# A decoder trunk on one core: another order for the opening of the projection

## The chip, the core and the metric

The kernel runs on one core of a Trainium2 chip. The core has a matrix engine (TensorE, PE in the profile), a vector engine (VectorE, DVE), an activation engine (ScalarE, ACT), GpSimd (POOL), and SyncE (SP), which here only issues DMAs. Each engine takes its own instructions in order and waits on semaphores for the others. Matrix results land in PSUM, of which the kernel uses eight banks of 128 x 512 numbers; all else is in SBUF, 128 partitions wide. The metric is the time of one execution on the device in microseconds (us); less is better.

## What is computed

One layer of a decoder trunk in float32. There are 1024 prompt tokens and 32 sample tokens (8 sequences of 4), 1056 in all, with 1024 features. Shortened from the reference:

```
h = x * rsqrt(mean(x*x) + eps) * norm_g              # RMSNorm, per token
b, c, u, z_a, v, z_b = split(h @ w_in)               # six parts of 512 columns
cu = c * u
y_a = b * conv3(cu) * silu(z_a)                      # short causal convolution, 3 taps
pooled = mean of the last 2/4/8/16 tokens of v - v   # four groups of 128 channels
y_b = (pooled @ pool_w) * pool_scale * silu(z_b)
x = x + concat(y_a, y_b) @ w_out
y = x * rsqrt(mean(x*x) + eps) * final_g
```

The last rows of cu and of v are given back as new states.

## The kernel before

**Layout.** In the projection, channels lie on partitions and the 1056 tokens along the free axis, in three column groups n0, n1, n2 of 352. The input x arrives transposed as raw[0], raw[1], raw[2], one tile for each group, with eight chunks of 128 features. RMSNorm's factor is one number per token, so it is not put on x: the projection takes the raw x, and its result is multiplied by R, a 128 x 1056 tile that holds the factor of each token in every partition (R2 is its square, for the product c * u).

**Three passes.** Every float32 operand is split into a high part (copied by ScalarE, type fp32r) and a low part (source minus high, by VectorE). A product is high x low + low x high + high x high, so a weight chunk takes three matmuls. `split` and `split2` (L153, L154) do this for x and for weights.

**Pairs.** The 24 blocks of 128 output channels are done as twelve pairs. Pair 0 (v and z_b of group 0) goes by plain matmuls, `project_first` (L188), into six banks pm[i, n] while x is still arriving. Each later pair p uses a Strassen-like scheme over n0 and n1 in `strassen`: blocks of twelve matmuls (`block`, L228) with the weight blocks B11, B21, B12, B22 and their combinations T1 to T4, against pieces of x (A11, A12, A22) and sums of them (S1 to S4). n2 is done plainly, into banks l and r. For pair 1 the tiles of the sums must first be made from raw[0] and raw[1] (S1f, S3f, S2f, S4f), and they take the buffers of raw_2 (S1), A21 (S3), raw_1 (S2) and raw_0 (S4). Weights are prepared pair by pair: `load_w` (DMA), `gain_w` (times norm_g, L202), `make_t` (T combinations, L207 to L209), and `make_unit` a (B11, B21), b (B12, B22), c (T1, T3) and d (T2, T4), each a split of 128 x 1024.

**The token factor.** The squared sums ss of the tokens come in two ways. For tokens 0 to 639, x is loaded once more with tokens on partitions (xk, five loads of 128 rows, `square`), and ScalarE squares and sums each row (`square2`, L239). For the other 416 tokens, `squares_head` and `squares_last` square raw[1] and raw[2] and add the chunks up in acc, and `sums_rest` sums over partitions with 128 x 1 matmuls (`rest`, L266), each copied into ss by ScalarE (L267). `rows` makes the inverse root (L274 to L280) and a diagonal tile diag of nine pieces (L285), and `rows_out` spreads it over the partitions with matmuls against ones (pr, L292) and copies it to R (L293) and R2 (L294). The heads of pair 0, in vb and szb, are multiplied by R from their banks (L531, L533).

**Order.** In the opening, a block marked `manual_schedule` fixes the order of PE, ACT, DVE and POOL among its own instructions, as they are written. All later instructions, and SP's queue throughout, are ordered by a planner: it plays the program through with estimated durations and lets each engine take the ready instruction that stands first in the program. Instructions written after the block can be placed between instructions of the block where its next one is not ready. The tile pools give buffers out by name: `tmp` has eight, the PSUM pool eight banks; an instruction that needs a buffer waits until all users of the one before are done.

After the projection the mixed rows go through w_out (L613, L685) and the final norm.

Of the kernel before, what the change touches and what calls it, by code (L numbers as in the profile page):

```python
# [7 lines left out]
F32 = mybir.dt.float32  # L8
# [5 lines left out]
P = 128  # L14
D = 1024
# [47 lines left out]
def trunk(ctx, tc, xt, xres, xct, w_first, w_in, w_out, pool_w, par, fg, sconv, spool,  # L63
# [166 lines left out]
                             skip_group_check=True)  # L230


    def square(t):
        xk = tp.tile([P, D], F32, tag="tmp", name=f"xk_{t}")
        nc.sync.dma_start(xk, xres[t * P:(t + 1) * P])
        return xk

    def square2(t, xk):
        nc.scalar.activation(xk, xk, AF.Square, accum_out=ss[:, t:t + 1])  # L239


# [6 lines left out]
        vt(sh[:, :2], sh[:, :2], sh[:, 2:4], op=ADD)  # L248
        vt(acc[:, :REST], sh[:, 0], sh[:, 1], op=ADD)

    def squares_last(acc):
        for k in range(0, KD, 2):
            sq = tmp(f"sq_{k}")
            nc.scalar.activation(sq[:, :2 * TN].rearrange("p (k c) -> p k c", k=2), raw[2][:, k:k + 2], AF.Square)
            if k == 0:
                vt(acc[:, REST:TC], sq[:, :TN], sq[:, TN:2 * TN], op=ADD)
            else:
                vt(sq[:, :TN], sq[:, :TN], sq[:, TN:2 * TN], op=ADD)
                vt(acc[:, REST:TC], acc[:, REST:TC], sq[:, :TN], op=ADD)

    def sums_rest(acc):
        pt = bank("rest")
# [6 lines left out]
    def rows():  # L269

        ms = sm.tile([P, NTOK], F32, tag="ms", name="ms")
        r = sm.tile([P, NTOK], F32, tag="r0", name="r0")
        u = sm.tile([P, NTOK], F32, tag="u0", name="u0")
        nc.vector.tensor_scalar(ms, ss, 1.0 / D, EPS, op0=ALU.mult, op1=ALU.add)  # L274
        nc.scalar.activation(u, ms, AF.Sqrt)
        nc.vector.reciprocal(r, u)
        nc.vector.tensor_tensor(u, ms, r, op=ALU.mult)
        nc.vector.tensor_tensor(u, u, r, op=ALU.mult)
        nc.vector.tensor_scalar(u, u, -0.5, 1.5, op0=ALU.mult, op1=ALU.add)
        nc.vector.tensor_tensor(r, r, u, op=ALU.mult)  # L280
        diag = tmp("diag")
        nc.vector.memset(diag[:, SEQ:], 0.0)
        for t in range(NTOK):
            m = min(P, TOK - t * P)
            nc.vector.tensor_scalar(diag[:m, t * P:t * P + m], ident[:m, :m],  # L285
                                    r[:m, t:t + 1], None, op0=ALU.mult)
        return diag

# [105 lines left out]

    def strassen(p, S1, S2, S3, S4, hooks):
        (q, j), (_, _) = PAIRS[p]
        if q == "v":
            left = vb[:, PM:]
            right = szb[j] = tmp(f"szb_{j}")
            scale = R  # L400
        elif q == "c":
            left, right = tmp(f"t_{j}"), tmp(f"um_{j}")
            scale = R2
        else:
            left, right = tmp(f"z_{j}"), tmp(f"y_{j}")
            scale = R
        n0, n1, n2 = cols

        def plain(i, name):
            pt = bank(name)[:, :TN]  # L410
            block(pt, p, ("B11", "B12")[i], pl[0], True, False)
            block(pt, p, ("B21", "B22")[i], pl[1], False, True)
            return pt

        a = bank(f"a_{p}")[:, :TN]
        block(a, p, "B11", A11, True, False)
        s1 = snap(f"s1_{p}")
        nc.scalar.copy(s1, a)
        if hooks.get("first"):
            block(a, p, "B21", A12, False, True)  # L420
            vt(left[:, n0], a, scale[:, n0], op=MUL)
            hooks["first"]()
        b = bank(f"b_{p}")[:, :TN]
        block(b, p, "T2", S2, True, False)
        t1 = snap(f"t1_{p}")
        vt(t1, b, s1, op=ADD)  # L426
        c = bank(f"c_{p}")[:, :TN]
        block(c, p, "T1", S1, True, False)
        if "plain" in hooks:
            pL, pR = hooks["plain"]  # L430
        else:
            pL = plain(0, f"l_{p}")
        vt(left[:, n2], pL, scale[:, n2], op=MUL)
        hooks["early"]()
        if not hooks.get("first"):
            block(a, p, "B21", A12, False, True)
            vt(left[:, n0], a, scale[:, n0], op=MUL)
        block(b, p, "T3", S3, False, False)
        t2 = snap(f"t2_{p}")
        vt(t2, b, s1, op=ADD)  # L440
        vt(right[:, n1], c, t2, op=ADD)
        if "plain" not in hooks:
            pR = plain(1, f"r_{p}")
        if q == "v":
            vt(right[:, n2], pR, R[:, n2], op=MUL)
        elif q == "c":
            vt(up[:, 2 + 2 * TN:], pR, left[:, n2], op=MUL)
        else:
            nc.scalar.copy(right[:, n2], pR)
        hooks["middle"]()  # L450
        block(b, p, "T4", A22, False, True)
        vt(left[:, n1], b, s1, op=ADD)
        gt(left[:, n1], left[:, n1], scale[:, n1], op=MUL)
        block(c, p, "B22", S4, False, True)
        vt(right[:, n0], c, t1, op=ADD)
        hooks["late"]()

        if q == "v":
            after_v(j)
            gt(right[:, both], right[:, both], R[:, both], op=MUL)  # L460
            silu(right)
        elif q == "c":
            gt(up[:, 2:2 + 2 * TN], right[:, both], left[:, both], op=MUL)
# [11 lines left out]
    with tc.manual_schedule(engines={ET.PE, ET.Activation, ET.DVE, ET.Pool}):  # L475
        for k in range(KD):
            prep_w0(k)
            split_x(2, k, 1)
            project_first(2, k)
        nc.vector.tensor_copy(gain.rearrange("p (k o) -> p k o", o=1), wfraw[:, :, 2 * P:])  # L480
        load_w(1)
        nc.sync.dma_start(part, par)
        sq = [square(t) for t in range(NTT)]
        for n in (0, 1):
            for k in range(0, KD, 2):
                split_x(n, k, 2)
            for k in range(KD):
                project_first(n, k)
        for i in range(2):
            nc.scalar.copy(heads[i][:, n2], pm[i, 2])  # L490
        acc = tmp("acc")
        squares_head(acc)
        gain_w(1)
        make_unit(1, "a")
        make_unit(1, "b")
        squares_last(acc)
# [3 lines left out]
        vt(S3f, raw[0][:, :KH], raw[1][:, :KH], op=ALU.subtract)  # L500
        S1 = xtile("xa", "S1")
        split(S1, S1f)
        S3 = xtile("xb", "S3")
        split(S3, S3f)
        for t in range(NTT):
            square2(t, sq[t])
        vt(S2f, S1f, raw[0][:, :KH], op=ALU.subtract)
        S4f = [tp.tile([P, 2, TN], F32, tag="tmp", name=f"S4f_{h}") for h in range(2)]
        for h in range(2):
            vt(S4f[h], raw[0][:, KH + 2 * h:KH + 2 * h + 2], S2f[:, 2 * h:2 * h + 2], op=ALU.subtract)  # L510
        S2 = xtile("xc", "S2")
        split(S2, S2f)
        make_t(1)
        make_unit(1, "d")
        pL = bank("l_1")[:, :TN]
        block(pL, 1, "B11", pl[0], True, False)
        block(pL, 1, "B21", pl[1], False, True)
        pR = bank("r_1")[:, :TN]
        block(pR, 1, "B12", pl[0], True, False)
        block(pR, 1, "B22", pl[1], False, True)  # L520
        sums_rest(acc)
        diag = rows()
        rows_out(diag)
# [4 lines left out]
        make_unit(1, "c")  # L528
        for n in (0, 1):
            for i in range(2):  # L530
                vt(heads[i][:, cols[n]], pm[i, n], R[:, cols[n]], op=MUL)  # L531
        for i in range(2):
            gt(heads[i][:, n2], heads[i][:, n2], R[:, n2], op=MUL)  # L533
    nc.sync.dma_start(scb[:, :, 0:2 * NB], sconv)
    nc.sync.dma_start(spb[:, :, 0:15 * NB], spool)
    pwraw = tmp("pwraw")[:, :NG * P].rearrange("p (g c) -> p g c", c=P)
    nc.sync.dma_start(pwraw, pool_w)

    linear = {}
    for p in range(1, NP):  # L540
# [17 lines left out]

        hooks = {"early": early, "middle": middle, "late": late}
        if p == 1:  # L560
            def first():
                split(pws, pwraw)
                after_v(0)
                silu(szb[0])

            hooks["plain"] = (pL, pR)
            hooks["first"] = first
        strassen(p, S1, S2, S3, S4, hooks)
        if PAIRS[p - 1][0][0] == "v":
            pool_linear(PAIRS[p - 1][0][1])  # L570
    nc.sync.dma_start(npool_p, npp)
# [213 lines left out]
```

## Time and profile before

| | |
|---|---|
| median of 3 runs | 401.23 us (399.94 to 402.31) |
| the profiled execution | 399.92 us |
| its span, first to last instruction | 397.9 us |
| mean granted TensorE clock | 0.967 |
| busy: PE, DVE, ACT, POOL | 371.4, 268.7, 174.1, 42.0 us |
| moved by DMA | 41.68 MB |

How to read the rows. A row of the timeline has the start in us, the duration in us, the engine, the line, the operation, the tile written and the tiles read, their sizes, and the count; a bracket gives the idle time of the engine just before and the instruction that ended it. Instructions that follow each other closely are merged in one row with their count. A row of a stretch has its limits, its length, then busy time and count of PE, PEld (weight loads), DVE, ACT and POOL, the granted clock as a part of full speed, the share of the DMA engines, and GB/s. A row of the waits has who waited for whom: us in all, times, the longest. PEclk on the page is the granted clock in tenths, in 40 slices of 9.95 us. The bracketed idle time of an engine matters only where that engine holds up the end.

### The profile page before, as it was taken

The page shows a single profiled execution, that of the slowest core. Times are in us where ns is not written, and L with a number is a line of the kernel's source. Part 1 is how long each engine was busy: PE and PEld are TensorE (multiplying, and loading weights), DVE is VectorE, ACT ScalarE, POOL GpSimd, SP SyncE. Part 2 cuts the span into 40 slices and gives each one's busy share as a digit, 9 for nine tenths or more (in the row PEclk, how much of TensorE's full clock was granted, in tenths as well). Part 3 has the DMA queues.
Part 4 walks back from the last instruction along what each step waited for, and adds up shares of the span by engine and source line. Part 5 has one row for each costly group of instructions (what it writes and reads, how often), then busy time and mean ns, then how long its engine had stood idle before and what let it go on. Part 6 is the DMA issues. An engine that isn't in the chain of part 4 may idle for free.

```text
span 397.9 us, 5295 instructions
## 1 busy us (share of the span) xinstructions
PE 371.4 (93%) x2114; PEld 353.8 (89%) x2114; DVE 268.7 (68%) x404; ACT 174.1 (44%) x297; POOL 42.0 (11%) x31
## 2 busy tenths in 40 slices
PE   9998058899999999999999999999999999999993
PEld 6898038899999999999999999999997889999883
DVE  4858848977587887657887766678339908322593
ACT  5884649425442545453353536163137606111211
POOL 0000001041003032000202200303301000000000
PEclk9999559899999999999999999999999999999999
DMA  7980030040402022040204041030808951400042
GB/s 221 413 308 0 1 133 0 0 161 0 161 0 100 7 77 85 2 160 2 105 2 160 0 152 38 24 136 5 321 6 279 413 225 53 161 0 2 1 171 105
DMA packets 13368, 41.68 MB, mean 105 GB/s; under 512 B 3744, under 2 KB 4896, under 8 KB 11936
## 3 DMA queue, kind: packets, MB, share of 16 engines
q1 hardware_dynamic: 13200, 41.02, 28.2%
q8 instruction: 16, 0.26, 0.3%
q10 hardware_dynamic: 144, 0.33, 0.2%
q14 instruction: 8, 0.07, 0.0%
HBM read 32.92 MB, written 8.42 MB: 104 GB/s over the span
## 4 chain that ended last, share of the span: by engine, by line
PE 74%; DVE 11%; ACT 7%; DMA 4%; issue 2%; SPq 1%; POOL 1%; DVEq 0%; ACTq 0%; POOLq 0%
PE b L228 14%; PE po L613 13%; PE pc L685 9%; PE r L228 9%; PE c L228 9%; PE a L228 9%; PE l L228 9%; DMA raw<-in_xt_dram 4%; PE pp L369 2%; DVE win L347 2%; ACT wraw L202 2%; ACT xk L239 1%; PE pr L292 1%; DVE tw L207 1%; DVE wa L154 1%
## 5 line engine op out<-in xcount | busy, mean ns | idle before, releaser
L613 PE MATMUL po<-wo,mix 128*128 128x512 f32 (+1 forms) x264 | 56.7, 375 | 0.2 <-DVE mix L154 0.2
L613 PEld LDWEIGHTS po<-wo,mix 128*128 128x128 f32 x264 | 46.2, 188 | 10.2 <-DVE mix L154 0.9
L228 PE MATMUL a<-A,wa 128*128 128x352 f32 x264 | 47.5, 329 | 0.0
L228 PEld LDWEIGHTS a<-A,wa 128*128 128x128 f32 x264 | 44.2, 192 | 0.6 <-ACT R L293 0.4
L228 PE MATMUL l<-pl,wa 128*128 128x352 f32 x264 | 44.5, 324 | 0.0
L228 PE MATMUL r<-pl,wb 128*128 128x352 f32 x264 | 44.5, 324 | 0.0
L202 ACT ACTIVATE wraw<-wraw,gain 128x256 f32<-128x256 f32 x88 | 36.7, 497 | 17.4 <-DMA wraw<-in_w_in_dram 16.4
L228 PEld LDWEIGHTS l<-pl,wa 128*128 128x128 f32 x264 | 43.0, 188 | 0.0
L228 PEld LDWEIGHTS r<-pl,wb 128*128 128x128 f32 x264 | 43.0, 188 | 0.0
L685 PE MATMUL pc<-mix,wo 128*128 128x416 f32 x192 | 36.5, 352 | 0.0
L685 PEld LDWEIGHTS pc<-mix,wo 128*128 128x128 f32 x192 | 35.9, 188 | 0.5
L207 DVE TENSOR_TENSOR tw<-wraw 128x1024 f32<-128x1024 f32 x11 | 14.1, 1280 | 20.9 <-ACT wraw L202 20.9
L228 PE MATMUL b<-S,wc 128*128 128x352 f32 x132 | 24.4, 336 | 2.6 <-DVE t L426 2.6
L153 ACT ACTIVATE wd<-tw 128x1024 fp32r<-128x1024 f32 x11 | 11.7, 1060 | 33.1 <-DVE tw L209 33.1
L228 PEld LDWEIGHTS b<-S,wc 128*128 128x128 f32 x132 | 22.6, 196 | 2.8 <-DVE t L426 2.8
L228 PE MATMUL b<-A,wd 128*128 128x352 f32 x132 | 23.2, 325 | 0.1
L228 PE MATMUL c<-S,wc 128*128 128x352 f32 x132 | 23.3, 324 | 0.0
L228 PE MATMUL b<-S,wd 128*128 128x352 f32 x132 | 23.1, 324 | 0.0
L228 PE MATMUL c<-S,wb 128*128 128x352 f32 x132 | 23.1, 324 | 0.0
L228 PEld LDWEIGHTS b<-A,wd 128*128 128x128 f32 x132 | 21.6, 188 | 0.4 <-DVE t L440 0.4
L228 PEld LDWEIGHTS c<-S,wc 128*128 128x128 f32 x132 | 21.7, 188 | 0.0
L228 PEld LDWEIGHTS b<-S,wd 128*128 128x128 f32 x132 | 21.7, 188 | 0.0
(173 smaller groups left out, 549.2 us busy)
## 6 DMA issues: line engine op xcount, KB each, us to landing
wraw<-in_w_in_dram SPq DMA_DIRECT2D x11, 1024.0 KB, 4.7
woraw<-in_w_out_dram SPq DMA_DIRECT2D x8, 512.0 KB, 5.9
raw<-in_xt_dram SPq DMA_DIRECT2D x4, 704.0 KB, 9.2
xk<-in_xres_dram SPq DMA_DIRECT2D x5, 512.0 KB, 10.8
zt<-in_xres_dram SPq DMA_DIRECT2D x5, 512.0 KB, 6.8
spill_b<-yb SPq DMA_DIRECT2D x4, 528.0 KB, 3.7
mixraw<-spill_b SPq DMA_DIRECT2D x4, 528.0 KB, 5.6
out_yt_dram<-zt SPq DMA_DIRECT2D x4, 512.0 KB, 2.8
```

The source lines that it names most:

```text
L153: nc.scalar.activation(hi, src, AF.Copy)
L154: nc.vector.tensor_tensor(lo, src, hi.bitcast(F32), op=ALU.subtract)
L202: nc.scalar.activation(t, t, AF.Copy, scale=gain[:, k:k + 1])
L207: nc.vector.tensor_tensor(t[:, 0:2], w[:, 2:4], w[:, 0::2], op=ALU.subtract)
L228: nc.tensor.matmul(pt, t[:, a, i, k * P:(k + 1) * P], x[:, b, k], start=first and s == 0, stop=last and s == len(seq) - 1, skip_group_chec ...
L239: nc.scalar.activation(xk, xk, AF.Square, accum_out=ss[:, t:t + 1])
L292: nc.tensor.matmul(pt, ones, diag[:, cols[n]], start=True, stop=True)
L347: nc.vector.tensor_tensor(o[:, lo2:PM + SEQ], a[:, lo2:PM + SEQ], a[:, lo2 - s:PM + SEQ - s], op=ALU.add)
L369: nc.tensor.matmul(pt[:, :TN], pws[:, a, g, :], pooled[g][b][:, cols[n]], start=(s == 0), stop=(s == 2))
L613: nc.tensor.matmul(pt, mix[k][:, b, t * P:(t + 1) * P], wo[k][:, a, c], start=(k == 0 and s == 0), stop=(k == KD - 1 and s == 2))
L685: nc.tensor.matmul(pt, wo[k][:, a, d * P:(d + 1) * P], mix[k][:, b, T0:], start=(k == 0 and s == 0), stop=(k == KD - 1 and s == 2))
```

## The change

It concerns the opening and pair 1 alone:

- The sums S1f and S3f come right after the splits of x, and S1, unit c and S3 ahead of S2 and unit d.
- `squares_head` stands ahead of the last x split; `squares_last` squares in three pieces into three buffers, and the additions (`sums_last`) are written after the manual block.
- The row squares are written after the block. Their first three loads go into R, R2 and up, which are not in use yet; the fifth is issued later.
- The banks of pair 0 are copied out unscaled by ScalarE, all six, and GpSimd multiplies the two heads by R in place, 1056 columns each.
- GpSimd makes diag instead of VectorE.
- The first bank of pair 1, a (24 matmuls), joins l and r (48) ahead of the column sums, inside the manual block; c with T1 is written ahead of b with T2.
- `sums_rest`, `rows` and `rows_out` are written after the block, and so are ordered by the planner.
- Splitting pool_w is written ahead of pair 1; `after_v(0)` and silu of szb[0] behind it.

```diff
+    def load_rows(t):
+        xk = {0: R, 1: R2, 2: up[:, 2:]}[t] if t < 3 else tmp(f"xk_{t}")
+        nc.sync.dma_start(xk[:, :D], xres[t * P:(t + 1) * P])
+        return xk[:, :D]
+    def square_rows(t, xk):
         nc.scalar.activation(xk, xk, AF.Square, accum_out=ss[:, t:t + 1])
...
+    def squares_last():
+        sq = []
+        for k in range(0, KD, 3):
+            t = tmp(f"sq_{k}").rearrange("p (k c) -> p k c", c=TN)[:, :min(3, KD - k)]
+            nc.scalar.activation(t, raw[2][:, k:min(k + 3, KD)], AF.Square)
+            sq.append(t)
+        return sq
+    def sums_last(acc, sq):
+        out = acc[:, REST:TC]
+        vt(sq[0], sq[0], sq[1], op=ADD)
+        vt(sq[0][:, :2], sq[0][:, :2], sq[2], op=ADD)
+        vt(out, sq[0][:, 0], sq[0][:, 1], op=ADD)
+        vt(out, out, sq[0][:, 2], op=ADD)
...
-        nc.vector.memset(diag[:, SEQ:], 0.0)
+        nc.gpsimd.memset(diag[:, SEQ:], 0.0)
...
-            nc.vector.tensor_scalar(diag[:m, t * P:t * P + m], ident[:m, :m],
+            nc.gpsimd.tensor_scalar(diag[:m, t * P:t * P + m], ident[:m, :m],
...
+        if p == 1:
+            a, s1, pL, pR = hooks["open"]
...
+        if p == 1:
+            block(c, p, "T1", S1, True, False)
         block(b, p, "T2", S2, True, False)
...
-        sq = [square(t) for t in range(NTT)]
+        xk = [load_rows(t) for t in range(4)]
+        acc = tmp("acc")
         for n in (0, 1):
             for k in range(0, KD, 2):
                 split_x(n, k, 2)
+                if (n, k) == (1, 4):
+                    squares_head(acc)
             for k in range(KD):
                 project_first(n, k)
...
         vt(S1f, raw[1][:, :KH], raw[1][:, KH:], op=ADD)
         vt(S3f, raw[0][:, :KH], raw[1][:, :KH], op=ALU.subtract)
+        gain_w(1)
+        make_unit(1, "a")
+        for i in range(2):
+            nc.scalar.copy(heads[i][:, n2], pm[i, 2])
+        sq = squares_last()
         vt(S2f, S1f, raw[0][:, :KH], op=ALU.subtract)
+        make_unit(1, "b")
         S4f = ...
+        make_t(1)
+        S1 = xtile("xa", "S1")
+        split(S1, S1f)
+        make_unit(1, "c")
+        S3 = xtile("xb", "S3")
+        split(S3, S3f)
+        for n in (0, 1):
+            for i in range(2):
+                nc.scalar.copy(heads[i][:, cols[n]], pm[i, n])
         S2 = xtile("xc", "S2")
         split(S2, S2f)
         make_unit(1, "d")
         S4 = xtile("xd", "S4")
...
+        pL, pR = plain1(0), plain1(1)
+        a1 = bank("a_1")[:, :TN]
+        block(a1, 1, "B11", A11, True, False)
+        s1 = snap("s1_1")
+        nc.scalar.copy(s1, a1)
+        block(a1, 1, "B21", A12, False, True)
+    sums_last(acc, sq)
+    xk.append(load_rows(4))
+    for t in range(NTT):
+        square_rows(t, xk[t])
+    sums_rest(acc)
+    diag = rows()
+    rows_out(diag)
+    for i in range(2):
+        gt(heads[i], heads[i], R, op=MUL)
...
+    split(pws, pwraw)
...
         strassen(p, S1, S2, S3, S4, hooks)
+        if p == 1:
+            after_v(0)
+            silu(szb[0])
```

More of the change, by code (lines that the diff above doesn't have):

```diff
@@ L230, in block @@
                              skip_group_check=True)
[L233 to L238, printed above, removed]
+    def load_rows(t):
[3 more added lines that the diff above has]
+    def square_rows(t, xk):
         nc.scalar.activation(xk, xk, AF.Square, accum_out=ss[:, t:t + 1])
@@ L249, in squares_head @@
         vt(acc[:, :REST], sh[:, 0], sh[:, 1], op=ADD)
[L251 to L259, printed above, removed]
+    def squares_last():
[11 more added lines that the diff above has]
+        vt(out, out, sq[0][:, 2], op=ADD)
     def sums_rest(acc):
@@ L413, in plain @@
             return pt
[L415 to L422, printed above, removed]
+        if p == 1:
+            a, s1, pL, pR = hooks["open"]
+        else:
+            a = bank(f"a_{p}")[:, :TN]
+            s1 = snap(f"s1_{p}")
+            block(a, p, "B11", A11, True, False)
+            nc.scalar.copy(s1, a)
         b = bank(f"b_{p}")[:, :TN]
+        c = bank(f"c_{p}")[:, :TN]
+        if p == 1:
+            block(c, p, "T1", S1, True, False)
         block(b, p, "T2", S2, True, False)
@@ L426, in strassen @@
         vt(t1, b, s1, op=ADD)
[L427 to L431, printed above, removed]
+        if p > 1:
+            block(c, p, "T1", S1, True, False)
+        if p > 1:
             pL = plain(0, f"l_{p}")
@@ L434, in strassen @@
         hooks["early"]()
-        if not hooks.get("first"):
+        if p > 1:
             block(a, p, "B21", A12, False, True)
-            vt(left[:, n0], a, scale[:, n0], op=MUL)
+        vt(left[:, n0], a, scale[:, n0], op=MUL)
         block(b, p, "T3", S3, False, False)
@@ L441, in strassen @@
         vt(right[:, n1], c, t2, op=ADD)
-        if "plain" not in hooks:
+        if p > 1:
             pR = plain(1, f"r_{p}")
@@ L486, in trunk @@
                 split_x(n, k, 2)
+                if (n, k) == (1, 4):
+                    squares_head(acc)
             for k in range(KD):
                 project_first(n, k)
[L489 to L496, printed above, removed]
         S1f, S3f, S2f = raw[1][:, KH:], raw[1][:, :KH], raw[0][:, :KH]
@@ L500, in trunk @@
         vt(S3f, raw[0][:, :KH], raw[1][:, :KH], op=ALU.subtract)
[L501 to L506, printed above, removed]
+        gain_w(1)
[3 more added lines that the diff above has]
+        sq = squares_last()
         vt(S2f, S1f, raw[0][:, :KH], op=ALU.subtract)
+        make_unit(1, "b")
         S4f = [tp.tile([P, 2, TN], F32, tag="tmp", name=f"S4f_{h}") for h in range(2)]
@@ L510, in trunk, with plain1 @@
             vt(S4f[h], raw[0][:, KH + 2 * h:KH + 2 * h + 2], S2f[:, 2 * h:2 * h + 2], op=ALU.subtract)
+        make_t(1)
+        def plain1(i):
+            pt = bank(f"lr{i}_1")[:, :TN]
+            block(pt, 1, ("B11", "B12")[i], pl[0], True, False)
+            block(pt, 1, ("B21", "B22")[i], pl[1], False, True)
+            return pt
+        S1 = xtile("xa", "S1")
[6 more added lines that the diff above has]
+                nc.scalar.copy(heads[i][:, cols[n]], pm[i, n])
         S2 = xtile("xc", "S2")
         split(S2, S2f)
-        make_t(1)
         make_unit(1, "d")
[L515 to L523, printed above, removed]
         S4 = xtile("xd", "S4")
@@ L527, in trunk @@
             split2(S4[:, 0, ks], S4[:, 1, ks], S4f[h])
[L528 to L533, printed above, removed]
+        pL, pR = plain1(0), plain1(1)
[13 more added lines that the diff above has]
+        gt(heads[i], heads[i], R, op=MUL)
     nc.sync.dma_start(scb[:, :, 0:2 * NB], sconv)
@@ L560, in trunk @@
         if p == 1:
[L561 to L567, printed above, removed]
+            hooks["open"] = (a1, s1, pL, pR)
         strassen(p, S1, S2, S3, S4, hooks)
+        if p == 1:
+            after_v(0)
+            silu(szb[0])
         if PAIRS[p - 1][0][0] == "v":
```

## The prediction, made before the changed kernel ran

> **What bounds the kernel now.** I read the page's engine and slice tables first, then busy time by stretch, TensorE's waits, and the timeline of each engine from 14 to 82 us.
>
> ```profile
> span 397.9 us, 5295 instructions
> ...
> PEclk9999559899999999999999999999999999999999
> ```
> ```profile
> 38.60:80.10 41.50, 23.00 (x106) 20.25 (x107) 32.73 (x57) 26.13 (x47) 1.86 (x2) 0.71 0.09 32
> 80.10:330.00 249.90, 249.59 (x1484) 242.78 (x1483) 175.59 (x226) 106.61 (x168) 38.73 (x22) 1.00 0.29 104
> ```
> ```profile
> PE rest L266 <- ACT ss L267: 13.3, 3, 12.8
> PE b L228 <- DVE t L426: 2.6, 1, 2.6
> PE pr L292 <- DVE diag L285: 2.5, 1, 2.5
> ```
> ```profile
> 34.55 4.04 PE L228 MATMUL r<-pl,wb 128*128 128x352 f32 x24
> 55.94 3.89 PE L292 MATMUL pr<-diag,ones 128*128 128x352 f32 x6 [2.54 <-DVE diag L285]
> 59.19 3.33 PE L228 MATMUL a<-A,wa 128*128 128x352 f32 x12
> 70.94 3.35 PE L228 MATMUL b<-S,wc 128*128 128x352 f32 x12 [2.55 <-DVE t L426]
> 80.14 2.10 PE L228 MATMUL a<-A,wa 128*128 128x352 f32 x12
> ```
>
> From 80 to 330 us TensorE is busy 249.6 of 249.9 us: nothing done there on another engine can pay. Everything lies between the end of r (34.55 + 4.04 = 38.59) and pair 2's first matmul at 80.14, 41.55 us. There three waits take 13.3 + 2.6 + 2.5 = 18.4. The rest of the loss is the clock: the stretch's mean is 0.71. pr took 3.89 at half clock, so 1.95 is lost; block a took 3.33 and block b 3.35 where a block of twelve takes 249.59 / 1484 x 12 = 2.02, so 1.3 each. Loss 18.4 + 1.95 + 2.6 = 23.0. Crosscheck: the work there is 7 blocks of 2.02, nine pp matmuls 1.5, pr 1.95 and the tiny `rest` ones, about 0.8: 18.4; 41.55 - 18.4 = 23.2. So **23 us is all there is to win**.
>
> Why TensorE stands still: the second `rest` matmul waits 12.8 us for a copy of a 128x1 column, and that copy stands on ScalarE behind an unrelated weight split.
>
> ```profile
> 28.97 0.79 ACT L254 ACTIVATE sq<-raw 128x704 f32<-128x704 f32 x1 [1.23 <-DVE acc L256]
> 39.47 1.04 ACT L239 ACTIVATE xk<-xk 128x1024 f32<-128x1024 f32 x1
> 50.30 1.06 ACT L153 ACTIVATE wd<-tw 128x1024 fp32r<-128x1024 f32 x1 [4.28 <-DVE tw L209]
> 53.61 0.17 DVE L274 TENSOR_SCALAR ms<-ss 128x9 f32<-128x9 f32 x1 [0.99 <-ACT ss L267]
> 55.20 1.80 DVE L285 TENSOR_SCALAR diag<-ident,r 128x128 f32<-128x128 f32 x9
> 57.51 0.45 ACT L293 COPY R<-pr 128x352 f32<-128x352 f32 x1 [1.56 <-PE pr L292]
> 60.62 1.07 ACT L294 ACTIVATE R<-R 128x1056 f32<-128x1056 f32 x1
> ```
>
> The split waits for tw, tw for VectorE, and VectorE lost time from 27 to 35 us: each of four squares waits about 1.2 us for the one free buffer. And no other matmul can go ahead, because by the code all eight banks are held: four pm accumulators until R exists, l, r, rest, pr.
>
> **The change part by part.** First the durations.
>
> ```profile
> 14.79 6.84 DVE L154 TENSOR_TENSOR A<-raw,A 128x704 fp32r<-128x704 f32 x8 [0.85 <-ACT A L153]
> 21.16 0.65 ACT L246 ACTIVATE sq_h<-raw 128x512 f32<-128x512 f32 x1
> 21.71 3.31 ACT L202 ACTIVATE wraw<-wraw,gain 128x256 f32<-128x256 f32 x8
> 26.14 1.23 DVE L154 TENSOR_TENSOR wa<-wraw,wa 128x1024 fp32r<-128x1024 f32 x1 [3.29 <-ACT wa L153]
> 36.46 1.63 DVE L500 TENSOR_TENSOR raw<-raw,raw 128x1408 f32<-128x1408 f32 x1
> 38.01 3.21 DVE L154 TENSOR_TENSOR S<-raw,S 128x1408 fp32r<-128x1408 f32 x2
> 38.18 1.38 ACT L153 ACTIVATE S<-raw 128x1408 fp32r<-128x1408 f32 x1 [0.28 <-DVE raw L500]
> 42.79 1.69 DVE L510 TENSOR_TENSOR S4f<-raw 128x704 f32<-128x704 f32 x2
> 47.60 1.22 DVE L207 TENSOR_TENSOR tw<-wraw 128x1024 f32<-128x1024 f32 x1
> 48.85 0.69 DVE L208 TENSOR_TENSOR tw<-wraw,tw 128x512 f32<-128x512 f32 x1
> 49.58 0.69 DVE L209 TENSOR_TENSOR tw<-wraw,tw 128x512 f32<-128x512 f32 x1
> 61.59 1.46 ACT L153 ACTIVATE S<-S4f 128x704 fp32r<-128x704 f32 x2
> 62.80 1.68 DVE L154 TENSOR_TENSOR S<-S4f,S 128x704 fp32r<-128x704 f32 x2
> ```
>
> *Sums first.* squares_head now stands ahead of the last x split: its square (0.65) and three small adds (about 0.9) move the A splits' end from 14.79 + 6.84 = 21.63 to 22.6; their matmuls come last in 30.7 us of queue, so this is hidden. S1f and S3f then end at 22.6 + 2 x 1.63 = 25.8 (before: 38.1). ScalarE: gain from 21.2, 3.3 to 24.5, unit a to 25.6, two copies 26.5, three squares without a buffer wait (two by the 1.04 row, one by 0.79) 29.4, unit b 30.4. VectorE: unit a 27.0, S2f 28.7, unit b (after ScalarE) 31.7, S4f 33.4, tw 2.6 to 36.0, S1 37.6, unit c 38.8, S3 40.4. S2 takes raw_1's buffer, free only then: high part 1.38 to 41.8, low part 43.4, unit d 44.7, S4 46.3. The order written out by hand sets all of that.
>
> *Accumulators copied unscaled.* Four copies by ScalarE (0.45 each) replace four VectorE multiplies (0.51 each), and free four banks near 40 us. So c, b and a can run before R is known. *Matmuls ahead:* a (24) joins l and r. TensorE: r ends 38.6, a's first half 40.6, c with T1 (S1 and unit c at 38.8) 42.6; then b with T2 has to wait for unit d at 44.7: a **gap of 2.1**. The second half of a waits for the copy of s1, which stands behind S4 on ScalarE: 43.4 + 1.46 + 0.45 = 45.4, so it can't fill the gap; `rest` fills about 0.7 of it. 1.4 stays.
>
> *Clock.* The wait of 2.55 us before block b above was followed by half clock, costing 1.3:
>
> ```profile
> 73.00:74.00 1.00, 1.00 (x5) 0.83 (x3) 1.00 (x2) 0.00 (x0) 0.00 (x0) 0.50 0.00 0
> ```
>
> I charge 1.3 again (0 at least; 2.6 were the next block slow too). The Trainium skill (TensorE: Matmul & The Clock Gate, "HAM oscillation — how this bites in real kernels") allows gaps up to about 3.4 us; by it the charge would be 0 and the time 1.3 less. The row here, a drop after 2.55, goes against it.
>
> *Row squares last, in R, R2 and up.* Five squares of 1.04 leave the chain ahead of S2; ScalarE idles from 31.8 (S1) to 36.0 (tw), where four fit. SP issues four loads instead of five at the old place; the fifth waits for a square's buffer (about 30 us, after the first two sum adds), and only load_w(2), pwraw and two state loads are queued near it, none wanted before 41. Hidden; without that cover the fifth costs a late R (below). The adds of sums_last, 3.1 by length, fit into VectorE's waits at 28.7 and 40.4.
>
> *R.* Column sums done near 46.7; to the first diag 55.20 - 53.61 = 1.6. Then nine diag pieces on POOL instead of VectorE, which no row shows on POOL; POOL's nearest rows:
>
> ```profile
> 1.01 0.29 POOL L132 TENSOR_SCALAR_AFFINE_SELECT ident<-ident 128x128 f32<-128x128 f32 x1
> 80.15 0.94 POOL L453 TENSOR_TENSOR t<-t,R 128x352 f32<-128x352 f32 x1 [17.90 <-DVE t L452]
> 80.46 1.72 DVE L154 TENSOR_TENSOR wb<-wraw,wb 128x1024 fp32r<-128x1024 f32 x1
> 81.17 2.57 POOL L463 TENSOR_TENSOR up<-um,t 128x704 f32<-128x704 f32 x1
> 88.08 2.46 POOL L390 TENSOR_TENSOR yc<-yc,R 128x1056 f32<-128x1056 f32 x1 [4.34 <-DVE yc L386]
> ```
>
> From 0.29 a piece (2.6 in all) to 0.94 (8.5); I take 0.4, nearest the piece of equal shape: 3.6, against 1.80. So diag ends near 52, R 53.2, R2 54.3. TensorE then still has pair 1's last two blocks, so R is wanted about when it comes. But pr's six matmuls stand in an in-order queue, planned by estimates: I charge 2.0 of waiting (0 to 8). The turn from b through t2 to the next b costs 0.5.
>
> These rows show POOL and VectorE holding each other up: wb took 1.72 instead of 1.23 beside POOL's 0.94, and the 704 multiply 2.57, more than the 1056 one. If each of the nine pieces waits out one VectorE operation of up to 1.2 us, R comes up to 8 later. That is the first rival. The Trainium skill (SBUF — State Buffer, "SBUF: two separate sides") says a POOL operation that reads SBUF and a VectorE one with two SBUF inputs lock each other out whole; these rows agree.
>
> *Heads by POOL* (two of 1056, 2.46 each, instead of 0.95 each) and after_v(0), silu and pws behind pair 1: only pp waits for them, and it can stand anywhere in pair 2. The 4.9 us stand in POOL's queue ahead of pair 1's own two multiplies, for which only after_u and, a pair later, y wait. Hidden; leaving pair 1 it also takes away the 2.6 wait for t L426.
>
> **Sum.** 23.0 lost before; 1.4 + 1.3 + 2.0 + 0.5 = 5.2 lost after: 17.8 gained. The profiled execution took 399.92 (span 397.9 and 2.0 around it): 382.1. The median of the runs is 1.3 higher, which gives 383.4; I take 382.7.
>
> **Rivals.**
> 1. *diag is held up on POOL, R late.* For: the rows above, with VectorE nearly full until 57. Against: adds that read a bank have but one SBUF input. Nine waits of up to 1.2 make R up to 8 late: 6 more than charged and again a slow clock, 388 to 391.
> 2. *VectorE becomes the bound.* It was busy 32.73 in the stretch; less diag 1.8 and multiplies 2.05 that is 29, and the stretch is to take 18.4 + 5.2 = 23.6, though 9 us of it is now done ahead of 38.6. If pair 2's units come 6 late: 389.
> 3. *Slower.* The fifth row load gets its buffer only when S4's splits end (46.3) and lands late: square 1.04, column root 1.6, diag, pr, R copies. TensorE would have no more than pair 1's blocks to do, 7 x 2.02 + 38.6 = 53, and then wait. Slower than before only if R comes 23 us after 53, hence a landing past about 65; at 3 us a load 49.5 is likelier, which costs 3. 401 to 403 if it decides.
> 4. *Nothing gained*, the planner's order putting rest and pr ahead of c and b, so that R still gates all: 401. But with R at 54 TensorE idles from 42.6 only 11.4 and 1.3 for the clock, about 390; 401 needs R near 65 here too.
>
> **How the numbers follow.** Forecast (376.9, no loss at all, to 387) 0.70; rival 1 0.13; rival 2 0.10; rival 3 0.04; rival 4 0.03. A measurement tells 0.5%, 2 us. The first three cases are faster: 0.93; same 0.03; slower 0.04. Range: 376.5, the whole loss gone, to 391, the top of rival 1.
>
> **What would show it.** Right: the `rest` wait gone; VectorE's S2 sum before 30 us; block c with T1 starting by 43; pair 2 starting near 60 instead of 80.14; clock near 1.0 throughout. Wrong: TensorE waiting at pr for a POOL diag (rival 1), at b or a of pair 2 for a VectorE split (rival 2), or ScalarE waiting for xk's DMA (rival 3); or a new wait behind 100 us.

## The result

| | before | after |
|---|---|---|
| median | 400.96 us (399.94 to 402.31, 4 runs) | 412.21 us (410.92 to 412.45, 4 runs) |
| the profiled execution | 399.92 us | 412.45 us |
| its span | 397.9 us | 410.7 us |
| mean granted TensorE clock | 0.967 | 0.956 |

The changed kernel takes 1.027 times as long (95% interval 1.0234 to 1.031). It is slower by 11.3 us, where 17.8 us less had been forecast. One of the runs of e5 below took 531.18 us at a granted clock of 0.649, a slow state, and is left out of its median. TensorE's waits show what was lost, its timeline where, and the chain behind the longest wait why.

TensorE's four largest waits after (us in total, times, longest):

```profile
PE pp L375 <- DVE pooled L154: 14.0, 1, 14.0
PE a L228 <- ACT s L540: 5.0, 1, 5.0
PE pr L298 <- POOL diag L291: 2.5, 2, 2.1
PE rest L272 <- ACT ss L273: 2.0, 3, 1.5
```

The `rest` wait of 13.3 us is down to 2.0, and b's wait for t from 2.6 to 0.6. In their place stand 5.0 us at a, and 14.0 us at pp, the nine matmuls of the pooled product, which waited 0.2 us before. Where these lie is seen in TensorE's timeline after:

```profile
32.61 3.98 PE L228 MATMUL lr<-pl,wa 128*128 128x352 f32 x23 [0.83 <-DVE wa L154]
41.28 2.10 PE L228 MATMUL a<-A,wa 128*128 128x352 f32 x12
45.04 0.38 PE L272 MATMUL rest<-ones,acc 128*128 128x1 f32 x2 [1.55 <-ACT ss L273]
51.58 3.89 PE L228 MATMUL a<-A,wa 128*128 128x352 f32 x12 [5.05 <-ACT s L540]
57.55 1.54 PE L298 MATMUL pr<-diag,ones 128*128 128x352 f32 x2 [2.08 <-POOL diag L291]
59.48 3.03 PE L298 MATMUL pr<-diag,ones 128*128 128x352 f32 x4 [0.40 <-POOL diag L291]
61.79 3.22 PE L228 MATMUL c<-S,wc 128*128 128x352 f32 x12
72.43 2.10 PE L228 MATMUL c<-S,wb 128*128 128x352 f32 x12
88.54 3.01 PE L375 MATMUL pp<-pooled,pws 128*128 128x352 f32 x9 [14.01 <-DVE pooled L154]
91.34 3.46 PE L228 MATMUL a<-A,wa 128*128 128x352 f32 x12
```

Pair 1's last block c ends at 72.43 + 2.10 = 74.53. Then TensorE stands still until 88.54, and pair 2 starts at 91.34; before, it started at 80.14. The rest after it is full but for the end of the kernel, which has its idle time in both kernels:

```profile
130.00:340.00 210.00, 209.69 (x1241) 203.35 (x1240) 148.18 (x190) 88.78 (x137) 31.76 (x18) 1.00 0.30 109
```

From pair 2's first block to the end the span takes 319.4 us (410.7 - 91.34), 317.8 before (397.9 - 80.14), and 1.4 of the 1.6 between them is that block's own slow clock. Nearly the whole difference therefore lies there and ahead of it. Loss by loss, counted as in the prediction, save that slow matmuls are set against the durations that later kernels show at full clock (2.10 for a block, 2.00 for six pr matmuls, 1.60 for nine pp):

| | forecast | after |
|---|---|---|
| l and r waiting for units a and b | 0 | 2.1 |
| `rest` | 0.7 hidden | 2.0 |
| gap beside a's second half | 1.4 | 5.0 |
| pr waiting for diag | 2.0 | 2.5 |
| turn b, t, b | 0.5 | 1.2 |
| slow clock on a 1.8, pr 2.6, c 1.1 | 1.3 | 5.5 |
| pp: wait 14.0, slow clock on it 1.4 and on pair 2's a 1.4 | 0 | 16.8 |
| sum | 5.2 | 35.1 |

Before, the loss was 23.0; 35.1 - 23.0 = 12.1, and the spans differ by 12.8. Without the row of pp the change would have lost 18.3 and gained about 5.

What pp waits for is a chain over four engines that starts at the end of block c. The timeline of VectorE, GpSimd and ScalarE after:

```profile
75.50 0.51 DVE L461 TENSOR_TENSOR um<-c,t 128x352 f32<-128x352 f32 x1
76.15 2.52 POOL L469 TENSOR_TENSOR up<-um,t 128x704 f32<-128x704 f32 x1 [1.66 <-DVE um L461]
78.71 1.15 ACT L389 ACTIVATE yc<-up,part 128x1024 f32<-128x1024 f32 x1 [5.01 <-POOL up L469]
79.89 1.28 DVE L392 SCALAR_TENSOR_TENSOR yc<-up,part,yc 128x1024 f32<-128x1024 f32 x1 [2.74 <-ACT yc L389]
81.10 1.22 DVE L358 SCALAR_TENSOR_TENSOR pl<-win,vb 128x1024 f32<-128x1024 f32 x1
82.23 1.28 DVE L392 SCALAR_TENSOR_TENSOR yc<-up,part,yc 128x1024 f32<-128x1024 f32 x1
83.65 2.41 POOL L396 TENSOR_TENSOR yc<-yc,R 128x1056 f32<-128x1056 f32 x1 [4.97 <-DVE yc L392]
83.72 2.36 DVE L365 TENSOR_TENSOR pl<-first,vb 128x1 f32<-128x1 f32 x1
86.11 1.08 ACT L153 ACTIVATE pooled<-pl 128x1056 fp32r<-128x1056 f32 x1 [3.99 <-DVE pl L365]
87.22 1.26 DVE L154 TENSOR_TENSOR pooled<-pl,pooled 128x1056 fp32r<-128x1056 f32 x1 [1.15 <-ACT pooled L153]
```

pl (L358), pp's own source, needs only vb, through win (L353, at 75.93). It stands in VectorE's queue behind the convolution's first sum (yc, L392), and that needs block c: c, um, up on GpSimd, yc on ScalarE, yc on VectorE. So in this order pp runs 14 us after c's end, even where R comes earlier (e2 and e3 below). Behind pp, in TensorE's in-order queue, stands all of pair 2, though its units were split by 75.6.

In the kernel before, VectorE did pl ahead of the convolution's sum and ahead of pair 1's last block c, which ran from 77.87, and pp waited 0.15 us:

```profile
69.06 1.22 DVE L352 SCALAR_TENSOR_TENSOR pl<-win,vb 128x1024 f32<-128x1024 f32 x1
74.44 1.65 PE L369 MATMUL pp<-pooled,pws 128*128 128x352 f32 x7 [0.15 <-DVE pooled L154]
84.96 1.28 DVE L386 SCALAR_TENSOR_TENSOR yc<-up,part,yc 128x1024 f32<-128x1024 f32 x1 [1.80 <-ACT yc L383]
```

### The profile page after: what moved, and what is told of

Its sections match the earlier page's. It is cut to its first block, busy times and chain, and to the rows that moved or that the text cites. A ratio compares the mean times of both kernels' runs of the same rounds, so it can differ in the third digit from the quotient of the medians.

```text
span 410.7 us, 5287 instructions
## 1 busy us (share of the span) xinstructions
PE 375.1 (91%) x2114; PEld 355.2 (86%) x2114; DVE 269.0 (66%) x387; ACT 175.0 (43%) x300; POOL 53.4 (13%) x41
## 4 chain that ended last, share of the span: by engine, by line
PE 73%; DVE 11%; ACT 6%; DMA 3%; POOL 3%; issue 2%; SPq 1%; DVEq 0%; POOLq 0%; ACTq 0%
PE b L228 14%; PE po L628 13%; PE pc L700 9%; PE a L228 9%; PE c L228 9%; PE r L228 9%; PE l L228 9%; DMA R<-in_xres_dram 2%; PE pp L375 2%; POOL diag L291 1%; ACT wraw L202 1%; DMA raw<-in_xt_dram 1%; DVE win L353 1%; DVE wb L154 1%; DVE S L154 1%
## 5 line engine op out<-in xcount | busy, mean ns | idle before, releaser
L628 PEld LDWEIGHTS po<-wo,mix 128*128 128x128 f32 x264 | 46.2, 188 | 10.2 <-DVE mix L154 0.8
L228 PE MATMUL a<-A,wa 128*128 128x352 f32 x264 | 49.4, 339 | 5.0 <-ACT s L540 5.0
L228 PEld LDWEIGHTS a<-A,wa 128*128 128x128 f32 x264 | 46.3, 200 | 5.1 <-ACT s L540 5.1
L202 ACT ACTIVATE wraw<-wraw,gain 128x256 f32<-128x256 f32 x88 | 36.6, 496 | 13.9 <-DMA wraw<-in_w_in_dram 12.9
L228 PE MATMUL l<-pl,wa 128*128 128x352 f32 x240 | 40.4, 324 | 0.0
L228 PE MATMUL r<-pl,wb 128*128 128x352 f32 x240 | 40.4, 324 | 0.0
L228 PEld LDWEIGHTS l<-pl,wa 128*128 128x128 f32 x240 | 39.1, 188 | 0.0
L228 PEld LDWEIGHTS r<-pl,wb 128*128 128x128 f32 x240 | 39.1, 188 | 0.0
L228 PE MATMUL c<-S,wc 128*128 128x352 f32 x132 | 24.2, 333 | 0.0
L228 PE MATMUL b<-S,wc 128*128 128x352 f32 x132 | 23.2, 324 | 0.6 <-DVE t L434 0.6
L228 PEld LDWEIGHTS b<-S,wc 128*128 128x128 f32 x132 | 21.6, 188 | 0.9 <-DVE t L434 0.9
```

The lines of the kernel that those rows point to most:

```text
L202: nc.scalar.activation(t, t, AF.Copy, scale=gain[:, k:k + 1])
L228: nc.tensor.matmul(pt, t[:, a, i, k * P:(k + 1) * P], x[:, b, k], start=first and s == 0, stop=last and s == len(seq) - 1, skip_group_chec ...
L628: nc.tensor.matmul(pt, mix[k][:, b, t * P:(t + 1) * P], wo[k][:, a, c], start=(k == 0 and s == 0), stop=(k == KD - 1 and s == 2))
```

## The experiments

Theory A, at first: pp is late because R is late, through diag and the heads on GpSimd. Theory B: each wait counts by itself. Theory C, formed after the first four runs: the order of VectorE's queue alone sets the time of pp.

**e1_pp_later.** The changed kernel, with pp written one pair later. Part of the computation is changed by it: the first two mix rows meet w_out's chunks in exchanged order, so its outputs are not the layer's, but the work is the same.

```diff
-        if PAIRS[p - 1][0][0] == "v":
+        if p == 2:
+            pool_linear(0)
+        if p > 1 and PAIRS[p - 1][0][0] == "v":
             pool_linear(PAIRS[p - 1][0][1])
```

> Undoes nothing of the opening; only the nine pp matmuls of pool group 0 are written behind pair 2 instead of behind pair 1. Theory A (TensorE's 14.0 us wait stands for pp alone, pair 2's weights are ready at 75.5 us at the latest): the wait goes, and with it the half-speed start after it (3.01 instead of 1.5 for pp, 3.46 instead of 2.02 for block a): 17 us less, about 395. Theory B (pair 2 could not have started earlier either, its weights or VectorE being late): less than 5 us, 407 or more.

Measured: 398.07 us, ratio to before 0.9931 (0.9907 to 0.9955). 14.1 us come back from moving nine matmuls (412.21 - 398.07), as much as pp's wait took, and pair 2 could start earlier, so this run's theory B (407 or more) falls. What is left of the change gains 2.9 us (400.98 - 398.07), less than the 5 us from the table, and the time is 3 us above this run's theory A (395); a wait at pair 2's b (3.1 us, for VectorE's t) is new. So the change is slower than the kernel before through pp.

**e2_diag_vector.** diag back on VectorE.

```diff
-            nc.gpsimd.tensor_scalar(diag[:m, t * P:t * P + m], ident[:m, :m],
+            nc.vector.tensor_scalar(diag[:m, t * P:t * P + m], ident[:m, :m],
```

> Only diag goes back from GpSimd to VectorE: 1.8 us instead of 7.39. Theory A (the end of pair 1 is set by pp, and pp by the chain R, heads on GpSimd, after_v on VectorE): R comes about 5.5 earlier and the whole chain to pp with it, about 407. Theory B (each wait is worth itself): only the 2.5 wait of pr and about 1 of clock go, 408.5; and if VectorE's load is what delays after_v, 410 to 412.

Measured: 412.66 us, ratio 1.0286 (1.0256 to 1.0316): no gain. The timeline of e2:

```profile
53.79 1.80 DVE L291 TENSOR_SCALAR diag<-ident,r 128x128 f32<-128x128 f32 x9
57.76 1.09 ACT L300 ACTIVATE R<-R 128x1056 f32<-128x1056 f32 x1
58.49 2.86 DVE L209 TENSOR_TENSOR tw<-wraw,tw 128x512 f32<-128x512 f32 x1
65.21 3.64 PE L228 MATMUL b<-S,wc 128*128 128x352 f32 x12 [4.08 <-DVE t L434]
71.52 2.10 PE L228 MATMUL c<-S,wb 128*128 128x352 f32 x12
87.38 3.01 PE L375 MATMUL pp<-pooled,pws 128*128 128x352 f32 x9 [13.76 <-DVE pooled L154]
```

R2 starts 5.3 us earlier than after (there at 63.03), and pr waits for nothing. But GpSimd's heads now run beside VectorE's weight work (tw takes 2.86 us, 0.69 in the kernel before), t comes late, b waits 4.1 us for it instead of 0.6 and then runs slow. So c ends only 0.9 us earlier, at 73.62, and pp still stands 13.8 us behind it. What the earlier R2 won was lost again at b, ahead of pp's wait. Theories A (407) and B (408.5) both missed; nearest came B's branch with VectorE's load as the delay, 410 to 412, though it is t that is late there and not after_v.

**e3_squares_held.** The first four row squares go back into the manual block, behind the split of S1.

```diff
         split(S1, S1f)
+        for t in range(4):
+            square_rows(t, xk[t])
         make_unit(1, "c")
...
-    for t in range(NTT):
-        square_rows(t, xk[t])
+    square_rows(4, xk[4])
```

> Only the first four row squares are written inside the fixed order, behind S1's high part, so that none can stand ahead of the last x split. ScalarE's 3.9 us wait for the load into R goes. Theory A: all that follows, R and pp included, moves up by about 4: 408. Theory B (the row squares had slack, only TensorE's own waits at l and r count): 2.2 less, 410.

Measured: 411.21 us, ratio 1.0264 (1.024 to 1.0287). In the profiled execution the waits of l and r are gone, a's wait is 2.3 instead of 5.0, and R2 starts at 58.24, 4.8 us earlier:

```profile
69.62 2.11 PE L228 MATMUL c<-S,wb 128*128 128x352 f32 x12
85.41 2.98 PE L375 MATMUL pp<-pooled,pws 128*128 128x352 f32 x9 [13.68 <-DVE pooled L154]
```

Of these 4.8 us, 2.8 are left at the end of c (71.73), because pr and b wait longer than after (3.8 and 1.7), and pp comes 3.1 earlier. This execution, 407.99 us, was the fastest of five; the median is only 1.0 us below that of the changed kernel, above both theories' times, and no trace of the other four shows why.

**e4_cb_ahead.** c with T1 and b with T2 inside the manual block, between the halves of a.

```diff
         nc.scalar.copy(s1, a1)
+        b1, c1 = bank("b_1")[:, :TN], bank("c_1")[:, :TN]
+        block(c1, 1, "T1", S1, True, False)
+        block(b1, 1, "T2", S2, True, False)
         block(a1, 1, "B21", A12, False, True)
```

> Only c with T1 and b with T2 are written inside the fixed order, between the halves of a, so that their two banks are given out ahead of pr's. Theory A: the 5.0 wait for s1 is filled, but three of the column sums now stand behind block b and a, so R and pp come later by 2 to 4 and the end with them: 412 to 416. Theory B: 24 matmuls fill the waits ahead of pr: 4 to 6 less, 407.

Measured: 412.74 us, ratio 1.0294 (1.0265 to 1.0322). c with T1 starts at 44.07 instead of 61.79, so its inputs did not hold it at 61.79; its place in the program did, behind pr, or the bank that it is given there, which this edit moves with it. But b now waits 2.7 us, by the program for S2's low part, done at 49.67; pr comes at 65.84, and pp waits 12.3.

These three move R or the blocks, and pp's wait stays 12 to 14 us. Theory A falls: with R2 5.3 us earlier (e2) pp moves by 1.2 us, with R's matmuls 8.3 us later (e4) by 1.6. The time of e4 lies in theory A's range, but not for its reason. Theory C names what the three left alone.

**e5_afterv_early.** after_v(0) and silu go back into pair 1, behind t1; pp stays where it was.

```diff
         vt(t1, b, s1, op=ADD)
+        if p == 1:
+            after_v(0)
+            silu(szb[0])
```

> pp keeps its place behind pair 1; only after_v(0) and silu are written further up, right behind the sum t1 of pair 1. Theory C (new, after the first four runs: VectorE's queue has the pooling's combine behind the convolution's first sum, which waits for ScalarE, GpSimd and so for the end of pair 1's block c; pp then always comes some 14 us after that block, whenever R comes): the 14.0 wait falls to 0 to 4, and 398 comes out, with up to 4 us given back by VectorE where the sums t stand behind the pooling. Theory A (R and the multiplies on GpSimd are what is late): 408 or more.

Measured: 401.97 us in the median, ratio 1.0023 (0.9991 to 1.0054). pp's wait is gone: pp runs inside pair 1, as it did before. 10.2 us come back (412.21 - 401.97), as theory C expected, not 14. The timeline of e5 shows where the rest goes:

```profile
66.05 2.46 POOL L553 TENSOR_TENSOR szb<-szb,R 128x1056 f32<-128x1056 f32 x1
66.13 3.47 DVE L353 TENSOR_TENSOR win<-vb 128x1038 f32<-128x1038 f32 x1 [7.80 <-POOL vb L553]
71.45 3.21 PE L228 MATMUL b<-S,wc 128*128 128x352 f32 x12 [3.38 <-DVE t L434]
75.28 3.89 PE L228 MATMUL b<-A,wd 128*128 128x352 f32 x12 [0.62 <-DVE t L449]
```

VectorE stands idle 7.8 us for GpSimd's first head, so here R's late coming does count. Beside GpSimd's second head, win then takes 3.47 us (1.23 in the kernel before); t stands behind it, TensorE waits 3.4 for t and then runs slow. That is the wait for t which the move of after_v(0) was to take away: the change traded 2.6 us of it for 14.0.

**c1_pp_squares** is e1 and e3 together (from here on w_out's first two chunks are taken as 0, 4, so the mix rows meet their own), **c2_pp_squares_diag** has e2's edit too.

> pp behind pair 2 (and the chunks of w_out in the order in which the mix rows are then finished), and the row squares held behind S1. Theory C: both gains add, since pp no longer hides what comes before it: 398 less the waits at l, r and s1 that holding the squares took away (2.5 + 2.8), 392 to 394. Theory A: the earlier opening again changes nothing, 398.

> As the one before, and diag on VectorE. Theory C: the waits of pr (3.8) and the slow blocks behind them go, but GpSimd's two multiplies then fall on VectorE's weight work and block b waits for t, as it did with diag alone changed (4.1): 389 to 393. Rival (GpSimd's 7.5 us for diag lay on the path in full): 386.

Measured: 395.67 us, 0.9876 (0.9834 to 0.9918), and 393.26 us, 0.9804 (0.9763 to 0.9845). c1 lies between the two theories' times, c2 0.3 above theory C's range. The edits that brought next to nothing with pp in its place now pay: e3's some 2 us (0.9931 - 0.9876 of 400), e2's 2.4 us (395.67 - 393.26). With pp out of the way, matmuls of pair 2's a stand in pair 1's waits: in c2 nine of them run just ahead of a wait for t of 2.9 us, where e2 waited 4.1. That this filling is the whole reason was not tested alone.

**c3_all** is c2 with a's first half and the copy of s1 written ahead of the split of S2, and c with T1 and b with T2 inside the block behind a.

```diff
+        block(a1, 1, "B11", A11, True, False)
+        s1 = snap("s1_1")
+        nc.scalar.copy(s1, a1)
         S2 = xtile("xc", "S2")
...
         block(a1, 1, "B21", A12, False, True)
+        block(c1, 1, "T1", S1, True, False)
+        block(b1, 1, "T2", S2, True, False)
```

> As the one before, and the copy s1 ahead of S2 on ScalarE, and c with T1 and b with T2 inside the fixed order behind block a. TensorE then has both halves of a and c to do while S2 and unit d are made, and R's matmuls come inside pair 1. Theory C: the waits for s1 (2.3 to 5) and for the column sums (2.4) go, with about 2 of half clock: 383 to 387, the time that was forecast for the change itself. Rival (VectorE is by now the bound of the opening): 389 to 392, no better than without this step.

Measured: 388.39 us, 0.9679 (0.962 to 0.9738), 1.4 us above the top of theory C's range and 0.6 below the rival's. TensorE's timeline of c3:

```profile
54.63 1.27 PE L228 MATMUL b<-A,wd 128*128 128x352 f32 x5 [2.90 <-DVE t L445]
55.70 3.45 PE L298 MATMUL pr<-diag,ones 128*128 128x352 f32 x6
83.61 3.89 PE L228 MATMUL b<-A,wd 128*128 128x352 f32 x12 [3.02 <-DVE t L445]
87.29 3.08 PE L228 MATMUL c<-S,wb 128*128 128x352 f32 x12
```

What is left are mainly two waits for VectorE's t, in this execution each followed by slow matmuls.

**c4_heads_vector** (c3 with the two multiplies of the heads on VectorE), **c5_pool_pair2** (c3 with after_v(0) and silu behind pair 2 and pp behind pair 3) and **c6_both** ask what holds VectorE there.

> As c3_all (388.39), with the two multiplies of the heads (vb and szb, 128x1056 each) on VectorE instead of GpSimd. Contention theory (GpSimd's heads stretch VectorE's own work: wb 3.20 for 1.22, swin 1.06 for 0.30, the two yc pieces 1.98 for 0.53, together 4.2 us too long, while the multiplies cost VectorE 2 x 1.26): VectorE ends its queue up to the second t 1.7 us earlier, 386 to 388. Rival (VectorE is the bound by its own work, the stretching lay beside idle time): 2.5 us of work more in its queue, 389 to 391.

> As c3_all (388.39), with after_v(0) and the silu of szb[0] written behind pair 2 instead of pair 1, and pp behind pair 3. Theory C carried on (in pair 2, b waits 3.0 us for its second t because VectorE has about 8 us of pooling and convolution ahead of it, and the matmuls behind the wait run at a lower clock: b 3.89 and c 3.08 for 2.10): that wait goes, 388.4 - 3.0 - 1.8 - 1.0 = 382.6, between 382 and 385. Rival (the wait moves on to pair 3, where VectorE has the same work ahead of pair 3's sums): 387 to 390.

> c4_heads_vector and c5_pool_pair2 together. Contention theory and theory C: 381 to 384, and no wait of TensorE over 3 us left but that before the six pr matmuls. Rival: VectorE's 2.5 us more delay pair 1's sums, so 384 to 388.

Measured: c4 387.73 us, 0.9687 (0.965 to 0.9724), which can't be told from c3, so the gain is not shown, though VectorE's own 2.5 us cost nothing either; c5 384.27 us, 0.9612 (0.9583 to 0.9642); c6 382.53 us, 0.9557 (0.953 to 0.9583), the fastest kernel of the study. Stretches of c6, and its waits:

```profile
38.00:60.00 22.00, 17.53 (x101) 15.62 (x100) 18.72 (x34) 17.06 (x35) 0.00 (x0) 1.00 0.14 55
60.00:100.00 40.00, 40.00 (x249) 40.00 (x248) 33.65 (x47) 21.12 (x36) 7.86 (x4) 1.00 0.19 67
```
```profile
PE b L228 <- DVE t L445: 3.3, 2, 2.9
PE a L228 <- ACT s L534: 0.5, 1, 0.5
PE b L228 <- DVE wd L154: 0.5, 1, 0.5
PE rest L272 <- ACT ss L273: 0.5, 2, 0.2
```

TensorE is busy all 40 us from 60 to 100, at full clock; 3.3 + 0.5 + 0.5 + 0.5 = 4.8 us of waits are left behind l and r.

**d2_before_afterv_late.** The test from the other side: the kernel before, with one part of the change alone.

```diff
                 split(pws, pwraw)
-                after_v(0)
-                silu(szb[0])
...
         strassen(p, S1, S2, S3, S4, hooks)
+        if p == 1:
+            after_v(0)
+            silu(szb[0])
```

> The kernel before, with one part of the change alone: after_v(0) and the silu of szb[0] are written behind pair 1 instead of inside it. Nothing else differs; ScalarE's row squares, the column sums, the diagonal and R stand as in the kernel before. Theory C (pp's time is set by VectorE's queue, where the pooling's sum then comes behind the convolution's first sum, and so behind the end of pair 1's block c): pp comes 12 to 14 us after c's end as in the changed kernel, the 2.6 us wait of b for t and its slow matmuls go, so 401 + 13 - 3 = 411, between 408 and 415. Rival (the other parts of the change, R's lateness above all, set the wait of pp, and this part alone is hidden): 399 to 403, pp waits less than 4 us.

Measured: 413.53 us, ratio 1.0345 (1.0317 to 1.0372). Rows of d2's timeline:

```profile
73.33 2.10 PE L228 MATMUL c<-S,wb 128*128 128x352 f32 x12
80.72 1.28 DVE L386 SCALAR_TENSOR_TENSOR yc<-up,part,yc 128x1024 f32<-128x1024 f32 x1
81.92 1.22 DVE L352 SCALAR_TENSOR_TENSOR pl<-win,vb 128x1024 f32<-128x1024 f32 x1
89.36 3.01 PE L369 MATMUL pp<-pooled,pws 128*128 128x352 f32 x9 [13.93 <-DVE pooled L154]
```

With vb scaled by VectorE as before and diag not on GpSimd, pl again stands behind yc, and pp waits 13.9 us behind c. This part alone costs 13.6 us, more than the whole change. Theory C stands, from both sides: the part put into the old kernel makes the loss (d2); in the changed one, pp moved out of the way (e1) or the part moved back (e5) takes away the wait.

## Why the prediction was wrong

**The step that failed** is the one it put as "Heads by POOL ... and after_v(0), silu and pws behind pair 1: only pp waits for them, and it can stand anywhere in pair 2. ... Hidden". Two things were wrong in it. pp does not stand anywhere: it is written right behind pair 1, ahead of pair 2, and in the planned queue it stayed there, so whatever delays pp delays all of pair 2. And the step asked what is queued behind the heads on GpSimd, but not what is queued ahead of pl on VectorE once after_v(0) is written behind pair 1: the convolution's chain, which hangs on the last block of pair 1. Priced at 0, it cost 13.6 us alone (d2) and 14.1 in the changed kernel (412.21 - 398.07). What the prediction should have followed is the moved step, on each queue that it was moved past.

**A second failure** stands beside it, in the sizes of the terms: ahead of pp the loss was 18.3 where 5.2 had been forecast (1.4 became 5.0, 1.3 became 5.5, and 2.1 came in at l and r), and with pp out of the way (e1) the change gains 2.9 us, not 17.8. Of the signs that the prediction named for being right, the `rest` wait fell to 2.0 us, but S2's sum starts at 32.48 instead of ending before 30, c with T1 starts at 61.79 instead of by 43, pair 2 at 91.34 instead of near 60, and the clock falls to 0.50 between 50 and 60 us. The paragraphs below take these terms one by one.

**Rival 3**, the only one on the slower side, had another place (the fifth row load); in the changed kernel the fifth row square started at 43.77 without a wait. ScalarE did wait for a row load, the sign named for this rival, but for the first one (below). The slower side was given 0.04 with no mechanism for pp in it.

**Rival 1** came true in its place, not in its weight. diag on GpSimd took 7.39 us for the nine pieces, near the 8.5 given as upper end, not the 3.6 taken:

```profile
53.52 7.39 POOL L291 TENSOR_SCALAR diag<-ident,r 128x128 f32<-128x128 f32 x9 [17.08 <-DVE r L286]
```

Taking it away gains nothing in the changed kernel (e2, where b's wait for t takes its place) and 2.4 us where pp is out of the way (c2 against c1).

**Row squares last**, "Hidden", was wrong. The prediction had them in ScalarE's idle time from 31.8; the planner put the first ahead of the last x split and the second ahead of unit a, and ScalarE even waited 3.89 us for the first one's load:

```profile
23.75 1.06 ACT L240 ACTIVATE R<-R 128x1024 f32<-128x1024 f32 x1 [3.89 <-DMA R<-in_xres_dram]
26.01 3.30 ACT L202 ACTIVATE wraw<-wraw,gain 128x256 f32<-128x256 f32 x8
29.21 1.05 ACT L240 ACTIVATE R<-R 128x1024 f32<-128x1024 f32 x1
```

The gain starts at 26.01, not at 21.2. Holding the squares back (e3, c1) takes away the 2.1 us at l and r and 2.7 of a's 5.0.

**Matmuls ahead.** The order "a's first half, c with T1, b with T2" did not come about. a's second half was queued next and waits for s1, whose copy stands behind S4 on ScalarE, and ran at 51.10 instead of ending at 45.4; c with T1, forecast to end at 42.6, started at 61.79 behind pr. So 1.4 became 5.0. Written into the block in the right order (c3) it ran at 43.27, and c3 gained 4.9 us over c2.

**Clock.** 1.3 was charged, 5.5 lost ahead of pp, because there were more and longer waits than forecast. The prediction's reading of the clock held in part: in e3 a block took 3.89 us behind a wait of 2.34, with the small `rest` matmuls and their waits just ahead, but not every wait is followed by a slow block (below).

**A reading** that was slightly off: of the four squares ahead of S1f three waited about 1.2 us for a buffer, not each of the four; no term rests on it.

**What was right.** TensorE loses 23 us between r and pair 2, and from 80 to 330 us next to nothing; sums first, unscaled accumulators and early matmuls can take most of that back. With pp, the squares, the order of the blocks, diag, and VectorE's queue put right, c6 has 4.8 us of waits left where 5.2 of loss were forecast, and its 382.53 us is the time that was forecast for the change. But c6 is another kernel, with parts that the change did not have, so that the two times meet confirms nothing about the change. What was forecast was at best the mechanism's worth, not what this order of instructions would let through.

## What to carry to other kernels

Where a step moves later in the program, follow it to the matmuls that use it, and ask what stands behind those matmuls in the in-order queue, and what will stand ahead of the step on its own engine: here nine matmuls that wait 14 us held up a pair whose operands were all ready. An operand that comes earlier pays only as far as the work that hangs on it can move: two edits that each made R2 some 5 us earlier hardly moved the median, because other waits ahead of pp grew (in e2, b's for t), and gave about 2 us each once pp was out of the way. To test a suspected part, put it alone into the old kernel as well as taking it out of the new one.

## What the runs showed of the hardware

GpSimd and VectorE hold each other up for whole instructions, even where VectorE's is tiny. In the chain above `pl<-first,vb`, one element on each partition, took 2.36 us: it began 0.07 us after GpSimd's yc and ended 0.02 us behind it. In the kernel before the same operation took 0.15. The Trainium skill (SBUF — State Buffer, "SBUF: two separate sides") describes an exclusive lock taken for the whole instruction by whichever starts first, between GpSimd and a VectorE operation with two SBUF inputs; this row agrees. In c3 a weight split of VectorE's (wb, 1.22 alone) took 3.20 beside the heads on GpSimd:

```profile
62.17 2.47 POOL L553 TENSOR_TENSOR szb<-szb,R 128x1056 f32<-128x1056 f32 x1
62.53 3.20 DVE L154 TENSOR_TENSOR wb<-wraw,wb 128x1024 fp32r<-128x1024 f32 x1
```

On VectorE the same multiply of a head took 1.24 us in c6, half of GpSimd's 2.47.

The clock after a wait of about 3 us is not one or the other. c3's wait of 3.02 was followed by a block of 3.89 us, its wait of 2.90 by five matmuls in 1.27 and then pr in 3.45 (1.07 and 2.00 in c6), while after e1's 3.10 the next block took 2.21 and after c6's 2.90 everything ran at full clock. Executions of one kernel differ too: of c3's four, one took 385.46 us at a mean granted clock of 0.996, one 389.88 us at 0.985. What decides it stays open.
